# A hybrid decoder step on one core: its two prompt mixers cut into steps that are queued between the dense products

## Chip, cores and metric

The kernel runs on one core of a Trainium2 chip. Its time is the device time of one execution in microseconds (us); three executions were timed. An execution under the hardware profiler gives the trace that is read here. PE is TensorE, DVE VectorE, ACT ScalarE, POOL GpSimd, and SP is the engine that issues the DMAs.

## The reference

One layer of a hybrid decoder on 1024 prompt tokens and 8 sample tokens (one new token each, behind 4096 cached ones). Width 1024, all float32.

```python
def decoder_layer(x, s0, past_k, past_v, lb, lam, lam_init, p):
    h = x + 0.5 * swiglu(rmsnorm(x, p['ffn1_norm']), p['ffn1_w_gate'], p['ffn1_w_up'], p['ffn1_w_down'])
    z = rmsnorm(h, p['mix_norm']) @ p['w_in']
    xq, xf, xi, xg, dq, dk, dv = jnp.split(z, IN_SPLITS, axis=-1)
    o_hg, s_new = hgrn2_mixer(xq, xf, xi, xg, lb, s0, p['hg_out_norm'])
    q = rmsnorm(dq.reshape(B, L, 2 * DA_HEADS, DA_HEAD_DIM), p['da_q_norm'])
    k = rmsnorm(dk.reshape(B, L, 2 * DA_HEADS, DA_HEAD_DIM), p['da_k_norm'])
    v = dv.reshape(B, L, DA_HEADS, DA_VDIM)
    ...
    o_da = rmsnorm(o_da, p['da_subln']) * (1.0 - lam_init)
    o = jnp.concatenate([o_hg.reshape(B, L, HG_WIDTH), o_da.reshape(B, L, DA_WIDTH)], axis=-1).astype(dt)
    h = h + o @ p['w_out']
    y = h + 0.5 * swiglu(rmsnorm(h, p['ffn2_norm']), p['ffn2_w_gate'], p['ffn2_w_up'], p['ffn2_w_down'])
    return y, k, v, s_new
```

The mixer has two halves: a gated linear recurrence (HGRN2, 4 heads of 128, in blocks of tokens with a running state), and causal differential attention (4 heads, two softmax maps each, whose difference weighs the values). The sample tokens attend to a paged cache of 4096 keys and values each, and have a recurrent state of their own. `swiglu` has an inner width of 2816.

## The kernel before, in words

**Dense products.** Each float32 product is made in three passes on float32r operands (high and low parts of weights and activations: `split`, L106). `mm3` (L376) keeps a weight tile in TensorE and streams 256, 264 or 512 columns of tokens; `dstep` (L431) is the same for the FFN's way down, and `units` (L498) the input projection, where tokens are stationary and 256 weight columns stream. The weights come in 678 tiles of 256 KB (`wtile`, `wload`); ACT makes the high part of each and DVE, or every second time POOL while `shared[1]` is set, the low part.

**Stages.** The prompt goes in two groups of 512 tokens, group 0 as two slices of 256 and 264 columns (the 8 sample tokens ride in the second). `first_half(grp)` is FFN 1 and the input projection (`win_phase`), whose results go to DRAM scratch by name: hk, hv, hg, hq for the recurrence, aq, ak, av for the attention. `mixer(grp)` is the work of one group in both mixer halves: four blocks of 128 tokens through `hgrn_block`, then sixteen (head, block) units of `attention`. `second_half(grp)` is the output projection, FFN 2 and the way out. In time: first half of group 0; first half of group 1 beside mixer 0; second half of group 0 beside mixer 1; second half of group 1 alone. The sample rows (`sample_stream`: per token 32 pages of keys, a softmax, 32 pages of values; then their recurrence) run beside all from the middle of the first input projection on.

**A block of the recurrence.** For each of 8 units (4 heads, two halves q of the decay levels) `stage1` makes decays with two 512-column matmuls (L666, L667), an exponential on ACT (L668), and two products on DVE (L672, L673); `stage2` makes 3 or 4 level products (L699, with L692 in the first half) that DVE copies into place (hAT, L701 and L708), and in the second half of a head goes on to the values and the state (L713, L714, L716; then ACT L717, DVE L721 on `hst`). The block ends with a norm (ACT L734, DVE L737 and L197, POOL L198, DVE L741 on `hln`) and four transposes (L744). The factor of that norm is a power, taken on POOL (L198).

**A unit of the attention.** Scores of two maps (L786; DVE L788 and L792, ACT L793), their weighted difference (DVE L795 to L798), transposes (L809; ACT L810), values (L814), a norm (ACT L817 and L818, DVE L821 on `aos`) and a last transpose (L823).

**PSUM.** Three banks `mm` for the dense products, two `mx` (decays, scores), two `my` (everything else of the mixers) and one `nm`. A matmul that begins a bank's next tile waits until the engines that read the tile before last in `mx` or `my` are through.

**What sets the order.** Every engine executes its instructions in one fixed order, that a list scheduler makes while the program is built. The program hands it the work by `weave`: after each piece of dense work, which yields its own cost, the side streams are advanced as far as their credit goes (cost times a rate: `R0`, `R1` for the mixers, `S0` to `S2` for the sample rows). Mixer instructions are handed over with a priority of 3000 (`hp(3000)`), with which the scheduler may put them ahead of dense work that was handed over before them.

```python
    sstream[1] = S1
    shared[1] = True
    rest = weave(first_half(1, SBs), [[mixer(0), R0, 3000], sstream])
    for s in rest:
        if s is not sstream:
            run(s[0])
    sstream[1] = S2
    rest = weave(second_half(0, HA), [[mixer(1), R1, 3000]] + [s for s in rest if s is sstream])
    for s in rest:
        run(s[0])
    shared[1] = False
    run(second_half(1, HB))
```

Of the kernel before, what the change touches and what calls it, by code (L numbers as in the profile page):

```python
# [18 lines left out]
P = 128  # L19
# [9 lines left out]
# columns of the constant table  # L29
# [4 lines left out]
def shape_constants():  # L34
# [5 lines left out]
    for l in range(7):  # L40
# [6 lines left out]
        # the columns of right halves alone  # L47
# [12 lines left out]
def kernel(ctx: ExitStack, tc: tile.TileContext, I, O):  # L60
# [74 lines left out]
    def load_consts():  # L135
# [3 lines left out]
        # lower bound: c1n = -(1 - lb) / 2 with lb the softmax over the two rows  # L139
# [13 lines left out]
        # lambda  # L153
# [11 lines left out]
        # gains of the mixers  # L165
# [18 lines left out]
    # rows of the sample tokens  # L184
# [15 lines left out]
    class Group:  # L200
        """tokens that pass the weights together: tiles as wide as the group"""
# [9 lines left out]
    class Slice:  # L211
        """columns of a group that one matrix product takes"""
# [53 lines left out]
    def norm_sums(sl):  # L266
        """sums of squares by block, down the partitions; the columns of each height"""
# [6 lines left out]
    def norm_spread(sl, R, r):  # L274
        """the factors along a row, on all partitions"""
# [23 lines left out]
    def scaled(gi, sl, d):  # L299
        """what norm_finish makes, but for the norm's factors: those come with the products' results"""  # L300
# [6 lines left out]
    def norm_row(sl):  # L307
        """the factors alone, along a row"""
# [41 lines left out]
    def wload(H, L, raw, src):  # L350
        # while DVE has the most to do, some of the low parts on Pool
# [7 lines left out]
    def wtile(src, c):  # L359
        """c columns of weights, from tiles of 512 / c blocks of rows: pairs of (high, low) parts"""  # L360
# [18 lines left out]
    FB = [2, 4, 4, 4, 4, 4]  # L379

    def ffn(pre, slices, done, deferred=False):
        wg, wu, wd = (I[pre + n] for n in ("_w_gate", "_w_up", "_w_down"))

        def gateup(f, hs):
# [6 lines left out]
            def gate(sl):  # L391
                pg = MM()
                mm3(pg, G, sl)
# [10 lines left out]
            def up(sl):  # L404
                pu = MM()
                mm3(pu, U, sl)
# [8 lines left out]
            # by slices where what comes before goes by slices  # L415
# [4 lines left out]
            for fn, sl in order:  # L420
                fn(sl)
                yield 0.01 * sl.w

        def dstep(W, m, hs, d, sl):
# [3 lines left out]
            for j in range(m):  # L428
                (H, L), (hH, hL) = W[j], hs[sl][j]
                for q, (a, b) in enumerate(((H, hH), (H, hL), (L, hH))):  # L430
                    PE.matmul(ps[:, :w], a[:, cs], b[:, :w], start=j == 0 and q == 0, stop=j == m - 1 and q == 2)  # L431
# [828 lines left out]
```

## Time and profile before

| | us |
|---|---|
| median of 3 executions (2468.16 to 2472.86) | 2472.05 |
| span of the profiled execution, first to last instruction | 2471.9 |
| PE busy (matmul) | 2304.7 |
| DVE busy | 1827.5 |
| ACT busy | 1071.8 |
| POOL busy | 999.5 |
| mean granted TensorE clock, share of full speed | 0.971 |

The profiled execution's own time is its span, 2471.9 us; nothing outside it is given, and it lies 0.15 us under the median. A matmul's end is modelled in the trace and matmuls overlap, so that a busy PE may still do less work than it could: the number of matmuls in a stretch of time says more than its busy share.

### The profile page before, as it was taken

The numbers are of one execution on the slowest core, as the hardware profiler recorded it, in microseconds if no ns is written. First come the engines' busy times: TensorE is split into PE (matmuls) and PEld (weight loads), VectorE is DVE, ScalarE is ACT, GpSimd is POOL, SyncE is SP. The second block draws the span as 40 slices with busy tenths as digits, with TensorE's granted clock in tenths as the row PEclk, the third lists the DMA queues.
The fourth block names the chain that finished last, engine by engine and source line by source line (L and its number), as shares of the span: only waits on it lengthen the run. The fifth ranks groups of instructions, "written<-read, shape, count | busy, mean of one in ns | idle before, by whom it ended". The sixth has DMA issues, their size and how long they took to land. (4 is left out here: it accounts for less than half of the span.)

```text
span 2471.9 us, 44310 instructions
## 1 busy us (share of the span) xinstructions
PE 2304.7 (93%) x15101; PEld 2079.1 (84%) x15101; DVE 1827.5 (74%) x3750; ACT 1071.8 (43%) x2465; POOL 999.5 (40%) x788
## 2 busy tenths in 40 slices
PE   7999999989998978989899879889798999999999
PEld 6999999989877866767888767677687889999999
DVE  6555657596799796798798997997987766555554
ACT  4322324435544434545554643434465554322222
POOL 4100101381176374474684673785756310100000
PEclk9999999999998998999899999999999999999999
DMA  4332334684466467576785773566755652332332
GB/s 137 90 95 83 112 91 125 183 286 139 130 217 205 134 213 230 165 234 215 239 280 145 243 236 114 186 211 202 235 173 182 183 170 94 90 95 91 90 95 74
DMA packets 273396, 402.37 MB, mean 163 GB/s; under 512 B 29641, under 2 KB 104650, under 8 KB 273170
## 3 DMA queue, kind: packets, MB, share of 16 engines
q1 hardware_dynamic: 273170, 399.54, 52.0%
q8 instruction: 119, 1.95, 0.3%
q14 instruction: 107, 0.88, 0.1%
HBM read 361.22 MB, written 38.21 MB: 162 GB/s over the span
## 5 line engine op out<-in xcount | busy, mean ns | idle before, releaser
L376 PE MATMUL mm<-xn,wH 128*128 128x256 f32 (+2 forms) x4800 | 1121.8, 327 | 19.4 <-DVE xn L106 5.7
L376 PEld LDWEIGHTS mm<-xn,wH 128*128 128x128 f32 x4800 | 808.6, 192 | 94.8 <-DVE xn L106 8.1
L376 PE MATMUL mm<-xn,wL 128*128 128x256 f32 (+2 forms) x2400 | 782.7, 326 | 1.4 <-DVE wL L106 1.4
L106 ACT CAST wH<-wr 128x512 fp32r<-128x512 f32 x672 | 409.3, 617 | 518.1 <-PE mm L376 275.3
L106 DVE TENSOR_TENSOR wL<-wr,wH 128x512 fp32r<-128x512 f32 x504 | 414.7, 825 | 163.8 <-ACT wH L106 132.8
L431 PE MATMUL mm<-h,wH 128*128 128x264 f32 (+2 forms) x2112 | 487.0, 324 | 7.3 <-DVE ft L409 4.7
L376 PEld LDWEIGHTS mm<-xn,wL 128*128 128x128 f32 x2400 | 461.1, 192 | 36.8 <-DVE wL L106 1.8
L954 POOL TENSOR_TENSOR kv<-kv,ss 128x512 f32<-128x512 f32 x256 | 371.2, 1459 | 145.3 <-DMA kv<-in_cache_k 127.1
L431 PEld LDWEIGHTS mm<-h,wH 128*128 128x128 f32 x2112 | 349.9, 190 | 38.4 <-DVE ft L409 5.8
L411 POOL TENSOR_TENSOR ft<-ft,acc 128x256 f32<-128x256 f32 (+1 forms) x110 | 101.5, 922 | 656.6 <-DVE ft L409 645.9
L431 PE MATMUL mm<-h,wL 128*128 128x264 f32 (+2 forms) x1056 | 340.5, 323 | 0.0
L498 PE MATMUL mm<-wH,xn 128*128 128x256 f32 (+1 forms) x1728 | 325.5, 286 | 7.2 <-ACT ez L527 2.5
L106 POOL TENSOR_TENSOR wL<-wr,wH 128x512 fp32r<-128x512 f32 x168 | 237.9, 1417 | 223.0 <-ACT wH L106 184.7
L1004 DVE SCALAR_TENSOR_TENSOR sacc<-kv,sS,sacc 128x128 f32<-128x128 f32 x480 | 283.5, 645 | 20.4 <-POOL sacc L1008 20.4
L498 PEld LDWEIGHTS mm<-wH,xn 128*128 128x128 f32 (+1 forms) x1728 | 259.4, 180 | 17.5 <-ACT ez L527 3.2
L1006 ACT ACTIVATE kv<-kv,sS 128x128 f32<-128x128 f32 x512 | 164.5, 391 | 210.3 <-DMA kv<-in_cache_v 161.2
L498 PE MATMUL mm<-wL,xn 128*128 128x256 f32 (+1 forms) x864 | 246.2, 286 | 1.0 <-DVE wL L106 1.0
L1008 POOL TENSOR_TENSOR sacc<-sacc,kv 128x512 f32<-128x512 f32 x128 | 185.6, 1450 | 117.9 <-issue 27.3
L433 DVE SCALAR_TENSOR_TENSOR xr<-mm,xr 128x264 f32<-128x264 f32 (+2 forms) x288 | 146.0, 511 | 91.4 <-PE mm L431 91.0
L431 PEld LDWEIGHTS mm<-h,wL 128*128 128x128 f32 x1056 | 200.2, 190 | 14.7
L955 DVE TENSOR_REDUCE sS<-kv 128x8 f32<-128x512 f32 x256 | 170.8, 673 | 37.2 <-POOL kv L954 36.8
L498 PEld LDWEIGHTS mm<-wL,xn 128*128 128x128 f32 (+1 forms) x864 | 155.2, 180 | 4.7 <-DVE wL L106 1.2
(219 smaller groups left out, 2409.0 us busy)
## 6 DMA issues: line engine op xcount, KB each, us to landing
kv<-in_cache_k SPq DMA_DIRECT2D x256, 256.0 KB
kv<-in_cache_v SPq DMA_DIRECT2D x256, 256.0 KB
wr<-in_ffn_w_gate SPq DMA_DIRECT2D x176, 256.0 KB
wr<-in_ffn_w_up SPq DMA_DIRECT2D x176, 256.0 KB
wr<-in_ffn_w_down SPq DMA_DIRECT2D x176, 256.0 KB
wr<-in_w_in SPq DMA_DIRECT2D x96, 256.0 KB
aq<-qt SPq DMA_DIRECT2D x64, 128.0 KB
wr<-in_w_out SPq DMA_DIRECT2D x32, 256.0 KB
```

Of the source, the lines that this page charges most:

```text
L106: return ACT.copy(H, src), (eng or DVE).tensor_tensor(out=L, in0=src, in1=H.bitcast(F32), op=ALU.subtract)
L376: PE.matmul(ps[:, :w], a, b[k][:, :w], start=k == 0 and j == 0, stop=k == n - 1 and j == 2)
L411: POOL.tensor_tensor(out=t, in0=t, in1=sl.acc, op=ALU.mult)
L431: PE.matmul(ps[:, :w], a[:, cs], b[:, :w], start=j == 0 and q == 0, stop=j == m - 1 and q == 2)
L433: DVE.scalar_tensor_tensor(out=sl.xr[d][:, :w], in0=ps[:, :w], scalar=0.25, in1=sl.xr[d][:, :w], op0=ALU.mult, op1=ALU.add)
L498: PE.matmul(ps[:tb, 0:256], a, b, start=k == 0 and j == 0, stop=k == KC - 1 and j == 2)
L954: POOL.tensor_tensor(out=kt, in0=kt, in1=qb, op=ALU.mult)
L955: DVE.tensor_reduce(out=Sb[:, i], in_=kt.rearrange("p (n d) -> p n d", d=64), op=ALU.add, axis=AX.X)
L1004: DVE.scalar_tensor_tensor(out=acc[:, hs], in0=vt[:, hs], scalar=w, in1=acc[:, hs], op0=ALU.mult, op1=ALU.add)
L1006: ACT.activation(vt[:, hs], vt[:, hs], AF.Copy, scale=w)
L1008: POOL.tensor_tensor(out=acc, in0=acc, in1=vt, op=ALU.add)
```

## The change

The same instructions are issued, as many of each kind on each engine. What changes is the order in which the program hands them to the scheduler, some buffers, and one constraint:

- `mm3` yields once more half way, so that a dense product of 8 weight blocks has two places for side work, and `newest` is the dense matmul handed over last.
- In `weave`, a stream with a priority (the mixers) may advance by one step per place only, and its TensorE instructions are held behind `newest` in TensorE's order (`issue_after`, an order without a semaphore).
- The mixers are one stream `mixers()` over both groups, from the middle of group 0's input projection on, with one fixed cost per step (`HSTEP`, `ASTEP`). `wait_for` makes a step give its place up until a result of the input projection has been handed over; the recurrence needs "hk" and "hq", then "hv", then "hg".
- A block of the recurrence goes in three stages, each a step behind the one before; a block's last transposes go into the next block (`behind`), and `hln` has two buffers. A unit of the attention goes in four steps, interleaved with the unit before it, and the last transpose of a unit comes with the unit after the next.
- In group 1's input projection hq comes second instead of fourth (`WORDER`).

```diff
     def mm3(ps, W, sl):
         w = sl.w
         n = len(W)
         for k, (H, L) in enumerate(W):
             for j, (a, b) in enumerate(((H, sl.xH), (H, sl.xL), (L, sl.xH))):
-                PE.matmul(ps[:, :w], a, b[k][:, :w], start=k == 0 and j == 0, stop=k == n - 1 and j == 2)
+                newest[0] = PE.matmul(ps[:, :w], a, b[k][:, :w], start=k == 0 and j == 0, stop=k == n - 1 and j == 2)
+            if 2 * k + 2 == n:
+                yield 0.005 * w
...
+    def wait_for(name, grp):
+        while (name, grp) not in made:
+            yield WAIT
+
+    WAIT = -1.0
...
-    WORDER = [("aq", "ak", "hk", "hq", "hv", "hg", "av"), ("hk", "hv", "hg", "hq", "aq", "ak", "av")]
+    WORDER = [("aq", "ak", "hk", "hq", "hv", "hg", "av"), ("hk", "hq", "hv", "hg", "aq", "ak", "av")]
...
-    def hgrn_block(b):
+    def hgrn_block(b, STEP):
...
-        osb = TT("hln", [P, 512], bufs=1)
+        while behind:
+            behind.pop(0)()
+        yield STEP
+        osb = TT("hln", [P, 512], bufs=2)
...
-            if q == 0:
-                return
+        def stage3(h):
+            hs = slice(h * P, (h + 1) * P)
+            AT = live[h]
             po = MY()
...
+        yield from wait_for("hv", b // 4)
+        hv = TT("hvt", [P, 512], bufs=1)
+        SP.dma_start(hv, hv_d[b])
         units = [(h, q) for h in range(4) for q in range(2)]
-        for i in range(len(units) + DEEP):
+        for i in range(len(units) + 2):
+            if i >= 3 and i % 2:
+                stage3((i - 3) // 2)
+            if 0 < i <= len(units):
+                stage2(*units[i - 1])
             if i < len(units):
                 stage1(*units[i])
-            if i >= DEEP:
-                stage2(*units[i - DEEP])
             if i == HEAD and b % 4 < 3:
                 hgrn_head(b + 1)
-            yield 2.0
+            if i == HEAD + 1:
+                yield from wait_for("hg", b // 4)
+                gate = TT("s512", [P, 512], bufs=2)
+                SP.dma_start(gate, hg_d[b])
+            yield STEP
...
     def attention(grp):
         att_consts()
-        pend = None
-        for h in range(4):
-            KT, V = att_load(h, grp)
-            for b in range(4 * grp, 4 * grp + 4):
-                a, tn = yield from att_scores(h, b, KT)
-                if pend is not None:
-                    yield from att_values(*pend)
-                pend = (h, b, V, a, tn)
-        yield from att_values(*pend)
+        units = [(h, b) for h in range(4) for b in range(4 * grp, 4 * grp + 4)]
+        U, kv_of = [], {}
+        for k in range(len(units) + 2):
...
+            if k > 1:
+                att_out(*U[k - 2])
+            if k < len(units):
+                att_scores(h, b, KT, qx, w, 0)
+            yield ASTEP[grp]
+            if 0 < k <= len(units):
+                att_turn(*U[k - 1])
+                yield ASTEP[grp]
+            if k < len(units):
+                att_scores(h, b, KT, qx, w, 1)
+                yield ASTEP[grp]
+            if 0 < k <= len(units):
+                att_values(*U[k - 1])
+                yield ASTEP[grp]
...
+    def mixers():
+        for grp in range(2):
+            yield from wait_for("hk", grp)
+            with tc.tile_pool(name=f"hg{grp}", bufs=1) as top[0]:
+                hgrn_consts()
+                for i in range(4):
+                    yield from hgrn_block(4 * grp + i, HSTEP[grp])
+            yield from wait_for("all", grp)
+            with tc.tile_pool(name=f"at{grp}", bufs=1) as top[0]:
+                yield from attention(grp)
+            mixed[0] = grp + 1
+            yield 0.1
+
+    HSTEP = (5.1, 4.8)
+    ASTEP = (2.9, 3.4)
...
                 credit[i] += c * s[1]
                 while credit[i] > 0:
-                    with hp(s[2]):
+                    with hp(s[2]), tc.issue_after(newest[0].ins) if s[2] else nullcontext():
                         n = next(s[0], None)
...
-                    credit[i] -= n
+                    credit[i] = 0.0 if n == WAIT else credit[i] - n
+                    if s[2]:
+                        break
...
+    mstream = [mixers(), 1.0, 3000]
+    weave(main, [mstream, sstream])
     sstream[1] = S1
     shared[1] = True
-    rest = weave(first_half(1, SBs), [[mixer(0), R0, 3000], sstream])
...
+    weave(first_half(1, SBs), [mstream, sstream])
+    while mixed[0] < 1:
+        next(mstream[0])
     sstream[1] = S2
-    rest = weave(second_half(0, HA), [[mixer(1), R1, 3000]] + [s for s in rest if s is sstream])
-    for s in rest:
+    for s in weave(second_half(0, HA), [mstream, sstream]):
         run(s[0])
```

**The order at two places.** TensorE's order at the end of mixer 0's recurrence, the last head of its fourth block, before (dense products, L376 and L431, stand where rows are left out). my is the pair of banks; hXR and hE are the factors of the levels, hvt the values, hAT what DVE assembles, hln the block's result.

```order
L692 MATMUL my<-hqt,hkT 128x128
L716 MATMUL my<-hst,hqd 128x128
L699 MATMUL my<-hXR,hE 128x64 x3
...
L699 MATMUL my<-hXR,hE 128x64 x4
...
L713 MATMUL my<-hvt,hkt 128x128
...
L714 MATMUL my<-hvt,hAT 128x128
L716 MATMUL my<-hst,hqd 128x128
...
L744 MATMUL my<-ident,hln 128x128 x2
```

The same place in the changed kernel (L710, L717, L732, L733, L735 and L776 are the lines that were L692, L699, L713, L714, L716 and L744):

```order
L733 MATMUL my<-hvt,hAT 128x128
L735 MATMUL my<-hst,hqd 128x128
L710 MATMUL my<-hqt,hkT 128x128
L717 MATMUL my<-hXR,hE 128x64 x3
...
L717 MATMUL my<-hXR,hE 128x64 x4
L732 MATMUL my<-hvt,hkt 128x128
...
L733 MATMUL my<-hvt,hAT 128x128
L735 MATMUL my<-hst,hqd 128x128
...
L776 MATMUL my<-ident,hln 128x128 x2
```

The kinds follow each other as before. Between the last L716 and the first L744 stood 54 dense products, and now 40; L732 stands right behind the four level products where some dense rows lay between.

TensorE's order where mixer 1's recurrence begins, in group 1's input projection, before (L644, L645 and L650 open a block; L498 is the projection, L376 with 512 columns its hq part):

```order
L498 MATMUL mm<-wL,xn 128x256
L498 MATMUL mm<-wH,xn 128x256
L644 MATMUL mx<-hgL,sufr 128x512
L645 MATMUL mx<-hgH,sufr 128x512
L650 MATMUL mx<-ident,hkt 128x128 x4
...
L376 MATMUL mm<-xn,wH 128x512 x2
```

And in the changed kernel:

```order
L376 MATMUL mm<-xn,wH 128x512 x2
...
L502 MATMUL mm<-wL,xn 128x256
L660 MATMUL mx<-hgL,sufr 128x512
L661 MATMUL mx<-hgH,sufr 128x512
L666 MATMUL mx<-ident,hkt 128x128 x4
...
L502 MATMUL mm<-wH,xn 128x256 x2
```

The block's opening stood ahead of hq and now stands behind it: 6724 dense products precede it before, 7014 after. The recurrence of mixer 1, from its first decays (L666, now L684) to its last, lay over 1438 dense products and now lies over 1148; the attention that follows it begins 10 us of dense work earlier than before and ends at the same place.

## Rows read from the trace of the kernel before

**Rows 1.** Windows, three stages: us, busy (instructions) by engine, TensorE clock, DMA share, GB/s.

```profile
0.00:425.00 425.00, 409.20 (x3352) 405.18 (x3353) 254.36 (x528) 148.45 (x311) 66.05 (x88) 1.00 0.34 103
425.00:2035.00 1610.00, 1464.20 (x8176) 1245.07 (x8174) 1334.43 (x2739) 784.64 (x1877) 896.97 (x652) 0.96 0.63 198
2035.00:2471.90 436.90, 431.28 (x3575) 428.83 (x3575) 238.68 (x484) 138.71 (x279) 36.49 (x48) 1.00 0.30 91
```

**Rows 2.** Windows of 50 us within the second and third stage, columns PE, PEld, DVE, ACT, POOL.

```profile
700.00:750.00 50.00, 40.98 (x167) 32.66 (x166) 49.66 (x87) 19.96 (x50) 37.71 (x28) 0.88 0.68 223
800.00:850.00 50.00, 50.00 (x257) 41.73 (x256) 33.32 (x86) 22.99 (x55) 13.22 (x11) 1.00 0.37 111
850.00:900.00 50.00, 42.10 (x192) 33.83 (x191) 50.00 (x86) 18.75 (x48) 36.23 (x26) 0.93 0.64 208
1450.00:1500.00 50.00, 40.05 (x163) 31.53 (x162) 50.00 (x78) 21.98 (x44) 32.77 (x21) 0.86 0.58 183
1600.00:1650.00 50.00, 41.68 (x175) 34.25 (x176) 50.00 (x87) 19.09 (x49) 40.89 (x29) 0.86 0.63 205
```

**Rows 3.** Waits of PE, whole span: waiting line <- releaser: us in total, times, longest.

```profile
PE my L744 <- DVE hln L741: 15.3, 11, 4.1
PE my L699 <- DVE hst L721: 10.9, 4, 5.4
PE mx L786 <- DVE atn L788: 10.7, 7, 3.4
PE my L823 <- DVE aos L821: 10.1, 7, 2.4
PE my L714 <- DVE hAT L708: 8.1, 5, 3.5
...
PE my L713 <- DVE hAT L708: 6.1, 5, 3.6
...
PE mx L786 <- DVE atn L792: 5.9, 1, 5.9
PE mx L786 <- DMA aKT<-kt: 5.3, 2, 4.0
...
PE my L692 <- DVE hAT L708: 4.2, 2, 3.8
...
PE my L699 <- DVE hE L673: 3.9, 4, 1.4
...
PE mx L666 <- ACT s L647: 3.1, 2, 2.7
```

**Rows 4.** Timeline, end of the fourth block: start us, us, engine, line [idle before <-releaser].

```profile
919.89 0.67 DVE L737 TENSOR_REDUCE tiny<-s 128x4 f32<-128x512 f32 x1
...
921.68 0.47 DVE L197 TENSOR_SCALAR tiny<-tiny 128x4 f32<-128x4 f32 x1
922.08 2.60 POOL L954 TENSOR_TENSOR kv<-kv,ss 128x512 f32<-128x512 f32 x2
924.64 1.06 POOL L198 TENSOR_TENSOR tiny<-tiny,mhalf 128x4 f32<-128x4 f32 x1
...
928.91 0.34 PE L744 MATMUL my<-ident,hln 128*128 128x128 f32 x1 [3.15 <-DVE hln L741]
```

**Rows 5.** Groups by line, DVE: count, busy us, mean ns, idle before.

```profile
L1004 DVE SCALAR_TENSOR_TENSOR sacc<-kv,sS,sacc 128x128 f32<-128x128 f32 x480 | 283.5, 645 | 20.4 <-POOL sacc L1008 20.4
L955 DVE TENSOR_REDUCE sS<-kv 128x8 f32<-128x512 f32 x256 | 170.8, 673 | 37.2 <-POOL kv L954 36.8
...
L708 DVE COPY_PREDICATED hAT<-masks,my 128x64 f32<-128x64 uint8 x224 | 54.0, 241 | 9.5 <-PE my L699 7.5
L673 DVE TENSOR_TENSOR hE<-hE,hkT 128x384 f32<-128x384 f32 x64 | 52.1, 814 | 0.0
L672 DVE TENSOR_TENSOR hXR<-hE,hqt 128x384 f32<-128x384 f32 x64 | 51.1, 799 | 2.5 <-DMA hqt<-hq 1.2 <-PE my L699 1.0
...
L741 DVE SCALAR_TENSOR_TENSOR hln<-hln,tiny,s 128x128 f32<-128x128 f32 x32 | 21.6, 733 | 1.3 <-POOL tiny L198 1.1 <-DMA hvt<-hv 0.2
```

More of the change, by code (lines that the diff above doesn't have):

```diff
@@ L392, in gate @@
                 pg = MM()
-                mm3(pg, G, sl)
+                yield from mm3(pg, G, sl)
                 t = sl.view(tt)
@@ L405, in up @@
                 pu = MM()
-                mm3(pu, U, sl)
+                yield from mm3(pu, U, sl)
                 t = sl.view(tt)
@@ L420, in gateup @@
             for fn, sl in order:
-                fn(sl)
-                yield 0.01 * sl.w
+                yield from fn(sl)
+                yield 0.005 * sl.w
         def dstep(W, m, hs, d, sl):
@@ L430, in dstep @@
                 for q, (a, b) in enumerate(((H, hH), (H, hL), (L, hH))):
-                    PE.matmul(ps[:, :w], a[:, cs], b[:, :w], start=j == 0 and q == 0, stop=j == m - 1 and q == 2)
+                    newest[0] = PE.matmul(ps[:, :w], a[:, cs], b[:, :w], start=j == 0 and q == 0, stop=j == m - 1 and q == 2)
             with hp():
@@ L497, in units @@
                     for j, (a, b) in enumerate(((xH, WH), (xL, WH), (xH, WL))):
-                        PE.matmul(ps[:tb, 0:256], a, b, start=k == 0 and j == 0, stop=k == KC - 1 and j == 2)
+                        newest[0] = PE.matmul(ps[:tb, 0:256], a, b, start=k == 0 and j == 0, stop=k == KC - 1 and j == 2)
                 with hp():
@@ L506, in win_phase @@
                 yield from win_queries(slices)
+                made.add((name, grp))
                 continue
@@ L513, in win_phase @@
                 yield None
+            made.add((name, grp))
         turn(0)
-    WORDER = [("aq", "ak", "hk", "hq", "hv", "hg", "av"), ("hk", "hv", "hg", "hq", "aq", "ak", "av")]
+        made.add(("all", grp))
+    made = set()
+    def wait_for(name, grp):
[3 more added lines that the diff above has]
+    WORDER = [("aq", "ak", "hk", "hq", "hv", "hg", "av"), ("hk", "hq", "hv", "hg", "aq", "ak", "av")]
     NEZ = 4
@@ new lines, in att_scores @@
+        tn = w["tn"]
+        sb = w[j] = TT(f"ap{j}", [P, KT.shape[2]], bufs=2 - j)
+        for pc in range(npc):
+            m = min(512, n - pc * 512)
+            ps = MX()
+            for x in range(2):
+                PE.matmul(ps[:, :m], qx[:, j, x], KT[:, j, pc * 512:pc * 512 + m], start=x == 0, stop=x == 1)
+            r0 = (7 - b) * P + pc * 512
+            DVE.tensor_tensor_reduce(out=sb[:, pc * 512:pc * 512 + m], in0=ps[:, :m], in1=negrel[:, r0:r0 + m],
+                                     op0=ALU.add, op1=ALU.max, scale=SLOPES[h], scalar=-3e38, accum_out=tn[:, 2 * j + pc:2 * j + pc + 1])
@@ L1049, in wout_phase @@
             ps = MM()
-            mm3(ps, W[d], sl)
+            yield from mm3(ps, W[d], sl)
             with hp():
@@ L1134, in first_half @@
             yield c
-            if then is not None and i > 50:
+            if then is not None and i > 58:
                 next(then, None)
@@ L1153, in second_half @@
         yield from ffn("ffn2", slices, out_step, grp == 1 or len(slices) == 1)
-    def mixer(grp):
-        with tc.tile_pool(name=f"hg{grp}", bufs=1) as top[0]:
-            hgrn_consts()
-            for i in range(4):
-                yield from hgrn_block(4 * grp + i)
-        with tc.tile_pool(name=f"at{grp}", bufs=1) as top[0]:
-            yield from attention(grp)
+    mixed = [0]
+    def mixers():
[12 more added lines that the diff above has]
+    ASTEP = (2.9, 3.4)
     def run(g):
```

104 lines of the change are left out of this document (50 added, 54 removed).

## The prediction

> **What bounds the kernel now.** First the windows by stage [rows 1]. In the first 425 us and the last 437 us TensorE is busy to 96 and 99% at full clock, and VectorE to 60 and 55%: these 862 us are TensorE's own work, and the change leaves them alone. The 1610 us between, in which mixers and sample rows run beside the dense products, are where it acts. [...]
>
> Second the windows of 50 us [rows 2], which show that this stage alternates. From 800 to 850 TensorE is full at clock 1.00 with 257 matmuls and VectorE busy for 33 us: TensorE bounds. From 700 to 750, 850 to 900, 1450 to 1500 and 1600 to 1650 VectorE is busy for 49.7 to 50 us, TensorE passes 163 to 192 matmuls only, and its clock is 0.86 to 0.93: VectorE bounds. The two changes of hand cost time, since what one engine has to spare in one stretch does not help the other in the next.
>
> Third, what TensorE waits for [rows 3]. The eleven rows sum to 83.6 us, and all are mixer matmuls. Nine wait for VectorE: for the block's norm (L744), for a PSUM bank that VectorE still reads (L699, L713, L692, L786), for the assembled levels (L714) or the attention's norm (L823). One waits for a DMA, one for ScalarE. Dense products hardly wait at all. So TensorE stands in its fixed order before a mixer matmul whose input is late, with dense work behind it that could run.
>
> **Why an input is late** is seen at one place [rows 4]. The fourth block's norm has its sum of squares at 922.15 us. The power, 1.06 us on GpSimd, begins at 924.64, because two products of the sample rows (2.60 us) stand ahead of it in GpSimd's order. The first transpose starts at 928.91 after 3.15 us of idling. The sample rows also hold VectorE for 283.5 + 170.8 = 454 us [rows 5]. A longer pipeline gives more cover against such a delay, but takes none of the work away.
>
> **The change, part by part.** Instructions and their counts are the same on every engine, the DMAs too, so no busy time is added or removed. I read from the order how much TensorE work stands between the matmul whose result is worked on and the matmul that waits, and call it cover: a product of 256 columns at 0.12 us (431.3 us for 3575 matmuls in the last stage [rows 1]), one of 512 at nearly twice that, less the work on the result that VectorE's own order holds, at its rows' durations.
>
> *Waits of the mixers.* The median cover grows by 1.5 us for L744, 0.3 for L699 behind the state, 1.2 for L713, 0.7 for L714 and L692, 1.0 for L823, 1.6 for the banks of L786 and by 3.4 for those of L666. If each wait becomes shorter by that, at most by its mean [rows 3], it is: L744 11 x 1.39 = 15.3; L699 4 x 0.3 = 1.2; L713 5 x 1.2 = 6.0; L714 5 x 0.7 = 3.5; L692 2 x 0.7 = 1.4; L823 7 x 1.0 = 7.0; L786 10.7; L666 3.1; together 48 us. The waits for the keys' DMA (5.3), for the one late L792 (5.9) and for hE (3.9; this cover gets shorter, from some 25 to 10 us, and stays long) are left as they are. 48 us is the upper bound; the lower is nothing. For nothing speaks that the four full windows alone hold 9.0 + 7.9 + 10.0 + 8.3 = 35.2 of the 145.8 us of idling [rows 2]: where VectorE is full, TensorE waits a little later instead. And the L744 cover does not grow everywhere: at the place shown, in 54 dense products before and 40 now, it shrinks; the spread over the eight blocks narrows from 4.1 to 16.2 us to 7.7 to 11.9 us. I take the middle, -24.
>
> [...]
>
> [...]
>
> *The second recurrence is squeezed.* Its start does not come earlier. The scheduler, with the mixers' priority, had already put it into the input projection; now hq stands ahead of it and it starts 40 us of dense work later, ending at the same place: 222 us of dense work before, 182 now. The four largest of its VectorE lines make 54.0 + 52.1 + 51.1 + 21.6 = 178.8 us for eight blocks [rows 5], 89 for its four. 89 x (1 - 182/222) = 16 us of VectorE work more must fit into the shorter stretch. VectorE is busy for 83% of the stage [rows 1], so there is room on average but not in a full window. Bounds 0 and +16; I take the middle, +8, as the stage is made of both sorts of windows. The attention of mixer 1 gets 10 us more and needs nothing.
>
> *What costs nothing.* The head of hgrn_block loads hv and the gate later, close to their use; of the loads into a block only hqt shows up as a wait, at 1.2 us on VectorE [rows 5], and it is now issued a step ahead of its use. Weight loads keep their higher priority on SP and pass no more mixer DMAs than before. load_consts and the sample rows keep their places: the sample softmaxes stand within 10 us of dense work of where they stood. The second buffer of hln hides the transposes' read; without it the next block's first copy would wait for them.
>
> The profiled execution took 2471.9 us, 0.15 under the median: 2471.9 - 24 - 7 + 8 = 2448.9, and so **2449 us** for the median.
>
> **Rivals.**
>
> *Nothing moves, since the scheduler had made this pipeline already.* For it: at the places looked at the kinds of TensorE matmuls follow each other as before, and where VectorE is full the order of TensorE decides nothing. [...] Against it: the lower quartile of most covers grows. Time 2472, within 5.
>
> *Slower: the squeezed recurrence meets a full VectorE.* The 16 us come in whole, and the waits stay: 2472 + 16 = 2488. It decides if VectorE is busy for 48 of 50 us or more all through mixer 1's recurrence, where it now is between full windows and others. For it also: three of the four longest covers of L744 lose 4.9, 4.3 and 3.0 us, and at the last of these three the norm was late [rows 4].
>
> *All covers work.* The waits fall by 48 and the clock by 21, the recurrence finds room: 2472 - 48 - 21 = 2403. For it: the five largest waits are short, 1.4 to 2.7 us in the mean, and a few products more would cover them. Against: the full windows.
>
> **How the numbers follow.** A measurement of this kernel can tell about 0.2%, 5 us, from no change. The forecast (2436 to 2466) has a chance of 0.38, the larger gain 0.17, no change 0.15, slower 0.30. The last is high because the share of work that VectorE gets in its busiest stretches is, by the order, not smaller than before. So faster 0.55, same 0.15, slower 0.30. The range goes from just above the larger gain's time to just above the slower rival's, 2405 to 2490; the forecast's own bounds, -48 - 21 and +16, lie at 2403 and 2488.
>
> **What would show it.** Right: in the middle stage TensorE's idle time falls from 146 to about 120 us; L744's successor L776 waits for less than 8 us in all and the waits of L786's successor L815 on L788's fall by half; the mean clock rises from 0.971 to about 0.975; VectorE's busy time stays at some 1830 us in a shorter span. Wrong: idling that only changes its line, full VectorE windows between 1080 and 1450 us (the second recurrence), or a first stage that is not the same to a few us. A new wait that the order does not show, as on SP behind a mixer load, would also make it wrong.

## The result, and the profile after

The changed kernel takes **2512.75 us** in the median of 4 runs (2512.1 to 2517.02), 1.0169 of the kernel before (95% interval 1.0155 to 1.0184): 41 us slower, where 23 us faster was forecast, and outside the range.

The windows by stage, of the changed kernel (columns as in [rows 1]):

```profile
0.00:425.00 425.00, 407.32 (x3330) 403.33 (x3331) 251.29 (x524) 147.04 (x309) 66.38 (x87) 1.00 0.35 103
425.00:2035.00 1610.00, 1443.29 (x7963) 1222.09 (x7962) 1315.69 (x2681) 764.10 (x1835) 895.51 (x649) 0.95 0.63 194
2035.00:2511.00 476.00, 468.25 (x3812) 461.55 (x3810) 263.64 (x547) 159.36 (x323) 39.09 (x53) 1.00 0.33 97
```

The first stage is nearly as before [rows 1]. In the second TensorE passes 7963 matmuls in the 1610 us that held 8176, and 237 are left over for the third. Over the whole program:

```profile
span 2511.0 us, 44330 instructions
PE 2318.9 (92%) x15101; PEld 2087.0 (83%) x15101; DVE 1830.6 (73%) x3750; ACT 1070.5 (43%) x2465; POOL 1001.0 (40%) x788
```

The 39.1 us of span are 14.2 us that the same 15101 matmuls are busy for longer (mean granted clock 0.967, not 0.971) and 24.9 us more in which TensorE idles (2511.0 - 2318.9 = 192.1, before 2471.9 - 2304.7 = 167.2). VectorE does the same work in nearly the same time. So both things that the change was to reduce have grown. In the middle stage TensorE idles for 166.7 us (1610 - 1443.29); before it was 145.8 (1610 - 1464.20 [rows 1]), and about 120 was forecast. The waits of that stage that VectorE ended went from 112 to 132 us, all rows summed. What TensorE waits for in the whole span now, the longest rows:

```profile
PE my L856 <- DVE aos L852: 23.4, 8, 6.2
PE mm L435 <- DVE xr L437: 15.0, 10, 3.8
PE my L717 <- DVE hst L740: 11.8, 6, 4.9
PE my L776 <- DVE hln L769: 10.5, 8, 3.0
PE my L717 <- DVE hE L691: 10.2, 6, 3.1
PE my L733 <- DVE hAT L726: 9.6, 5, 3.9
PE mx L815 <- DVE atn L817: 8.6, 5, 2.4
PE my L732 <- DVE hAT L726: 6.7, 8, 2.1
```

Against [rows 3], the block's norm (L776, before L744) fell from 15.3 to 10.5 us and the scores' bank (L815, before L786) from 10.7 to 8.6. But the attention's last transpose (L856, before L823) went from 10.1 to 23.4, hE (now L717 behind L691) from 3.9 to 10.2, and a dense product, L435 of the FFN's way down, now waits 15.0 us; the answering row of before, L431 behind L433, had 2.0. The releaser is VectorE in all of them. The wait of L692 for hAT, 4.2 us, is gone.

**One such wait.** The longest, in the first attention; start, length, engine, line (of VectorE's queue the pieces behind 1259.68 us):

```profile
1260.54 0.28 ACT L849 ACTIVATE s<-my 128x128 f32<-128x128 f32 x1
1260.71 0.20 ACT L849 ACTIVATION_READ_ACCUMULATOR s<-my 128x1 f32 x1
```

```profile
1259.68 2.68 DVE L1058 SCALAR_TENSOR_TENSOR sacc<-kv,sS,sacc 128x128 f32<-128x128 f32 x4
1262.28 0.68 DVE L106 TENSOR_TENSOR wL<-wr,wH 128x512 fp32r<-128x512 f32 x1
1262.88 1.76 DVE L478 SCALAR_TENSOR_TENSOR ft<-ft 128x512 f32<-128x512 f32 x1
1264.57 0.14 DVE L197 TENSOR_SCALAR tiny<-atn 128x1 f32<-128x1 f32 x1
...
1265.22 2.48 DVE L1058 SCALAR_TENSOR_TENSOR sacc<-kv,sS,sacc 128x128 f32<-128x128 f32 x4
1267.63 0.67 DVE L1009 TENSOR_REDUCE sS<-kv 128x8 f32<-128x512 f32 x1
1268.22 1.06 DVE L852 TENSOR_SCALAR aos<-aos,tiny 128x128 f32<-128x128 f32 x1
```

```profile
1264.05 1.71 POOL L1008 TENSOR_TENSOR kv<-kv,ss 128x512 f32<-128x512 f32 x1
1265.73 0.59 POOL L198 TENSOR_TENSOR tiny<-tiny,mhalf 128x1 f32<-128x1 f32 x1
```

```profile
1269.43 0.45 PE L856 MATMUL my<-ident,aos 128*128 128x128 f32 x1 [6.18 <-DVE aos L852]
```

The sum of squares is there at 1260.91 us. The three steps that lead from it to `aos` take 0.14, 0.59 and 1.06 us, 1.8 in all, but they end at 1269.28, 8.4 us later: sample rows (L1008, L1009, L1058), a weight's low part (L106) and a pass over the queries of the dense hq product (L478) stand ahead of them in the queues of VectorE and GpSimd. TensorE comes to L856 with dense work behind it and idles for 6.18 us.

**Where along the program.** The dense products' matmuls (L376, L435 and L502, before L376, L431 and L498) are as many in both kernels, so time can be compared at the same count of them, from the start of each in the trace. Time of each kernel less that of the kernel before, in us; the last three columns are runs of the next section. A single wait just ahead of a count (the longest in the rows above is 6.2 us) moves its row:

| dense matmuls begun | before at | changed | finer weaving alone | rate 0.9 for pair 1 | changed, pace 1.6 |
|---|---|---|---|---|---|
| 4200 | 562 | +7.3 | +1.1 | -1.3 | +7.9 |
| 5700 | 965 | +11.3 | +3.2 | -6.2 | +12.0 |
| 6150 | 1102 | +1.7 | +0.5 | -5.8 | +10.2 |
| 6850 | 1252 | +33.9 | +12.0 | -7.5 | +22.3 |
| 7380 | 1358 | +17.4 | +9.2 | -8.1 | +26.2 |
| 7635 | 1414 | +17.6 | +12.2 | +12.6 | +22.8 |
| 8605 | 1743 | +41.5 | +27.7 | +20.3 | +38.5 |
| 9335 | 1997 | +38.8 | +26.2 | +19.6 | +34.6 |
| 9570 | 2052 | +39.1 | +27.6 | +16.7 | +26.0 |

A difference at one count is also a difference of place: at 6850 the changed kernel has just ended its first attention (last transpose at product 6849, before 6573) and not yet begun its second recurrence, which before had begun at 6750. Of the 39 us of span, 24 come between products 7635 and 8605, where the second pair of mixers meets the sample rows. That stretch, of the kernel before (972 dense matmuls) and of the changed one (975):

```profile
1413.90:1743.00 329.10, 291.14 (x1303) 232.15 (x1302) 295.52 (x547) 142.41 (x333) 219.16 (x153) 0.94 0.62 196
```

```profile
1431.80:1787.80 356.00, 303.16 (x1355) 240.42 (x1353) 322.01 (x594) 147.82 (x343) 232.95 (x162) 0.94 0.60 188
```

VectorE is busy for 90% in both, and the stretch is longer by 27 us with 26.5 us more of VectorE's work in it, at the same clock. Of that work 19 us are the sample rows' multiply-adds and reductions (L1004 and L955 before, L1058 and L1009 now: 104.5 and 123.6 us). The order has put it there.

### The profile page after: what moved, and what is told of

It reads as the page before. It is cut to its first block, busy times and chain, and to the rows that moved or that the text cites. A ratio compares the mean times of both kernels' runs of the same rounds, so it can differ in the third digit from the quotient of the medians.

```text
span 2511.0 us, 44330 instructions
## 1 busy us (share of the span) xinstructions
PE 2318.9 (92%) x15101; PEld 2087.0 (83%) x15101; DVE 1830.6 (73%) x3750; ACT 1070.5 (43%) x2465; POOL 1001.0 (40%) x788
## 5 line engine op out<-in xcount | busy, mean ns | idle before, releaser
L376 PE MATMUL mm<-xn,wH 128*128 128x256 f32 (+2 forms) x4800 | 1125.4, 329 | 18.6 <-DVE xn L106 6.6
L376 PEld LDWEIGHTS mm<-xn,wH 128*128 128x128 f32 x4800 | 813.0, 193 | 93.9 <-DVE xn L106 8.3
L376 PE MATMUL mm<-xn,wL 128*128 128x256 f32 (+2 forms) x2400 | 787.1, 328 | 0.0
L106 ACT CAST wH<-wr 128x512 fp32r<-128x512 f32 x672 | 409.8, 617 | 572.1 <-PE mm L376 317.6
L106 DVE TENSOR_TENSOR wL<-wr,wH 128x512 fp32r<-128x512 f32 x504 | 419.1, 834 | 174.2 <-ACT wH L106 139.7
L435 PE MATMUL mm<-h,wH 128*128 128x264 f32 (+2 forms) x2112 | 487.9, 325 | 21.3 <-DVE xr L437 15.0
L376 PEld LDWEIGHTS mm<-xn,wL 128*128 128x128 f32 x2400 | 463.5, 193 | 35.9
L1008 POOL TENSOR_TENSOR kv<-kv,ss 128x512 f32<-128x512 f32 x256 | 372.4, 1463 | 148.7 <-DMA kv<-in_cache_k 125.8
L435 PEld LDWEIGHTS mm<-h,wH 128*128 128x128 f32 x2112 | 350.3, 190 | 54.4 <-DVE xr L437 20.3
L435 PE MATMUL mm<-h,wL 128*128 128x264 f32 (+2 forms) x1056 | 342.5, 325 | 0.0
L502 PE MATMUL mm<-wH,xn 128*128 128x256 f32 (+1 forms) x1728 | 328.1, 288 | 9.0 <-DVE ez L558 2.3
L106 POOL TENSOR_TENSOR wL<-wr,wH 128x512 fp32r<-128x512 f32 x168 | 239.2, 1424 | 242.7 <-ACT wH L106 210.6
L1058 DVE SCALAR_TENSOR_TENSOR sacc<-kv,sS,sacc 128x128 f32<-128x128 f32 x480 | 284.7, 647 | 20.7 <-POOL sacc L1062 20.7
L502 PEld LDWEIGHTS mm<-wH,xn 128*128 128x128 f32 (+1 forms) x1728 | 261.6, 182 | 18.3 <-DVE ez L558 2.9
L502 PE MATMUL mm<-wL,xn 128*128 128x256 f32 (+1 forms) x864 | 247.6, 287 | 1.9 <-POOL wL L106 1.0
L435 PEld LDWEIGHTS mm<-h,wL 128*128 128x128 f32 x1056 | 200.7, 190 | 14.9
L1009 DVE TENSOR_REDUCE sS<-kv 128x8 f32<-128x512 f32 x256 | 170.4, 674 | 41.3 <-POOL kv L1008 41.3
L502 PEld LDWEIGHTS mm<-wL,xn 128*128 128x128 f32 (+1 forms) x864 | 156.7, 182 | 5.4 <-POOL wL L106 1.5
```

The costliest lines, as they stand in the source:

```text
L106: return ACT.copy(H, src), (eng or DVE).tensor_tensor(out=L, in0=src, in1=H.bitcast(F32), op=ALU.subtract)
L376: newest[0] = PE.matmul(ps[:, :w], a, b[k][:, :w], start=k == 0 and j == 0, stop=k == n - 1 and j == 2)
L435: newest[0] = PE.matmul(ps[:, :w], a[:, cs], b[:, :w], start=j == 0 and q == 0, stop=j == m - 1 and q == 2)
L502: newest[0] = PE.matmul(ps[:tb, 0:256], a, b, start=k == 0 and j == 0, stop=k == KC - 1 and j == 2)
L1008: POOL.tensor_tensor(out=kt, in0=kt, in1=qb, op=ALU.mult)
L1009: DVE.tensor_reduce(out=Sb[:, i], in_=kt.rearrange("p (n d) -> p n d", d=64), op=ALU.add, axis=AX.X)
```

## The experiments

Two theories first. Theory 1: VectorE's full windows make the loss, so less VectorE work removes it. Theory 2: the finer, paced pipeline itself costs. Differences are to runs of the kernel before on the same chip; the ratio's interval stands with each.

**Less work on VectorE**, in the kernel before and in the changed one; both leave out every second multiply-add of the sample values:

```diff
-                    DVE.scalar_tensor_tensor(out=acc[:, hs], ...
+                    if i % 4 == 0:
+                        DVE.scalar_tensor_tensor(out=acc[:, hs], ...
```

> The kernel before, without every second of the multiply-adds that VectorE does on the sample rows' values (256 of 480 at 0.645 us, 165 us of VectorE work; their pages' share is left out of the result). Theory 1 (full VectorE: the change moved VectorE work from stretches with room into stretches where VectorE has none, and the time followed it): the span falls by 60 to 140 us, since VectorE is no longer full. Theory 2 (the finer pipeline itself costs: more steps, each with a wait of its own): this kernel falls too, by some tens of us; what tells the theories apart is the distance to its twin.

> The changed kernel without the same 256 multiply-adds of VectorE (165 us; that share of the sample values is left out of the result). Theory 1: the distance to the kernel before with the same cut falls from 40 us to under 15. Theory 2: it stays between 30 and 50 us.

Measured: 2426.4 us (ratio 0.9806, 0.9785 to 0.9827) and 2469.4 us (0.9976, 0.9963 to 0.9989). With some 100 us of VectorE's busy time gone both gain 43 to 48 us, and the distance between them stays at 43. VectorE's work is worth half its length here, but it isn't the total that the change suffers from: theory 1 falls in this form.

**Undoing one part of the changed kernel.** The old order of the weights, and slower recurrence with faster attention:

```diff
-... ("hk", "hq", "hv", "hg", "aq", "ak", "av")]
+... ("hk", "hv", "hg", "hq", "aq", "ak", "av")]
```

> The changed kernel with group 1's input projection in the order of before (hk, hv, hg, hq). The second recurrence then begins some 13 us of dense work later still, ends 40 later, and the attention behind it is pressed into 190 instead of 232 us of dense work. Theory 1: the recurrence is less dense and the attention denser, whose VectorE work has room: 2500 to 2515. Theory 2: nothing changes, 2510 to 2516. A third theory, that the moved hq is what costs: back to 2475 to 2485.

```diff
-    HSTEP = (5.1, 4.8)
-    ASTEP = (2.9, 3.4)
+    HSTEP = (5.1, 5.6)
+    ASTEP = (2.9, 2.8)
```

> The changed kernel with other step costs for the second mixer alone: 5.6 instead of 4.8 for the recurrence, 2.8 instead of 3.4 for the attention. The second recurrence then lies over 230 instead of 192 us of dense work (237 before the change). Theory 1: the stretch from the output projection on, which took 27 us more, gives back half or more: 2485 to 2500. Theory 2: the pipeline is the same, 2508 to 2517.

Measured: 2523.7 us (1.0199, 1.0175 to 1.0223) and 2514.6 us (1.0162, 1.0141 to 1.0182). The early hq is not the cause: without it the changed kernel is 7 us slower by the ratios, 1.0199 and 1.0169, whose intervals overlap. With other rates the loss at product 8605 is 20 us in place of 42, but by product 9570, with the attention, it is 41. So a theory of one stretch alone falls.

Then faster hand-over, the old steps, and the old sequence of two stages:

```diff
-    mstream = [mixers(), 1.0, 3000]
+    mstream = [mixers(), 1.6, 3000]
```

> The changed kernel, with the mixers handed over 1.6 times as fast (1.6 units of their work for each unit of dense work, and not 1.0); the steps and their order inside a block or unit are as changed. By the order of TensorE the second recurrence then stands in 990 to 1149 us of dense work (changed: 1006 to 1198) and its attention ends at 1466 (changed: 1483). Theory A, the slow hand-over costs (mixers late, steps of one block too close together in dense work): most of the 40 us come back, 2470 to 2490. Theory B, the new steps themselves cost (second stage handed over before the next first stage, half scores, the late turn): no change, 2505 to 2520.

> The changed kernel with the steps of the kernel before inside the recurrence and the attention (hgrn_block and attention as they were, with waits for hq, hv and hg ahead of each block), the rest as changed: hand-over beside the input projection, one step per place, new order of the weights. Their costs are divided by the rates of the kernel before (0.55 and 0.8), so that they are handed over as fast as there. Theory A, start and pace of the hand-over cost: it stays slow, 2495 to 2520, since the first recurrence still starts at 543 us of dense work (changed 512, before 470). Theory B, the new steps cost: back to 2460 to 2480.

```diff
-            if 0 < i <= len(units):
-                stage2(*units[i - 1])
             if i < len(units):
                 stage1(*units[i])
+            if 0 < i <= len(units):
+                stage2(*units[i - 1])
```

> The changed kernel with one pair exchanged in the recurrence: the first stage of a unit is handed over before the second stage of the unit before it, as in the kernel before, and not after it. Theory B in its narrow form, the shorter way from the first stage to the second (cover for hE some 10 us and not 25) costs: the waits of the level products fall from 25.5 us towards 15 and the time by 10 to 20 us, 2492 to 2503. Theory A, pace and start: the scheduler moves little, 2507 to 2517.

Measured: 2500.1 us (1.0103, 1.0077 to 1.0130), 2509.0 us (1.0129, 1.0106 to 1.0153) and 2518.2 us (1.0161, 1.0136 to 1.0187). The pace is worth some 16 us by the ratios (1.0169 and 1.0103), 13 by the two spans; the old steps don't bring the old time back; the narrow theory of hE falls. In the run with pace 1.6 the three waits that had grown are shorter:

```profile
PE my L856 <- DVE aos L852: 11.1, 9, 3.2
...
PE my L717 <- DVE hE L691: 7.2, 4, 4.4
...
PE mm L435 <- DVE xr L437: 7.0, 8, 1.9
```

but the scores' bank and the block's norm wait longer again:

```profile
PE mx L815 <- DVE atn L817: 18.5, 16, 2.5
PE my L776 <- DVE hln L769: 17.4, 11, 3.8
```

The first three give back 23.3 us and the other two take 16.8. Nine of the table's 13 us come at the end, where the last attention ends 124 dense products earlier (its last transpose at product 9382, changed 9506). The stretch from product 9350 to about 9600, changed and with pace 1.6:

```profile
2041.70:2093.80 52.10, 48.83 (x346) 44.67 (x345) 29.57 (x76) 25.72 (x60) 1.65 (x3) 1.00 0.54 162
```

```profile
2038.20:2082.10 43.90, 42.15 (x299) 38.61 (x298) 22.27 (x43) 15.13 (x32) 0.55 (x1) 1.00 0.58 174
```

**One part alone, in the kernel before, and two parts undone.** hq second (the diff above, reversed):

> The kernel before with one part of the change alone: in the second input projection the queries of the recurrence (hq) come second and not fourth. In the changed kernel this part was worth 11 us (2523.7 without it, 2512.7 with it). By the order the second recurrence then stands in 964 to 1146 us of dense work (before 962 to 1199) and its attention ends 26 us earlier. Theory A, an early start and an early end of the mixers are what counts: faster, 2455 to 2468. Theory B, what is packed denser costs: 182 us of dense work for the second recurrence as in the changed kernel, so slower than 2480.

Changed kernel with pace 1.6 and the old order of the weights:

> The changed kernel with two parts undone: the mixers handed over 1.6 times as fast, and hq fourth in the second input projection as before. Only the new steps inside blocks and units, the weaving by single steps and the start of the first recurrence (517 us of dense work, before 501) remain; by the order both attentions then end where they ended before (941 and 1483). Theory A, pace (some 15 us by the run with the faster hand-over) and the early hq (13 us by the kernel before with that part alone) make the loss: 2473 to 2490. Theory B, the steps cost: the distance of the run with the faster hand-over stays or grows, 2495 to 2520.

New steps alone:

> The kernel before with one part of the change alone: the new steps of the recurrence and of the attention (second stage before the next first stage, third stage apart, scores by halves, turn and way out a unit later, loads close to their use). Hand-over, weaving and the order of the weights are as before. By the order the scheduler then runs the steps more quickly: second stages of the first recurrence in 501 to some 685 us of dense work (before 501 to 730), its attention ends at 914 (before 941), the second one at 1474 (before 1484). Theory B, the steps cost by themselves: 2495 to 2520. Theory A, only pace and place cost: within 2465 to 2485; by the packing of VectorE (the recurrence of group 0 in 45 us less of dense work) at the upper end or some 10 us above.

Finer weaving alone (also the two counts of places, 80 to 150 and 50 to 58, as in the change):

```diff
+            if 2 * k + 2 == n:
+                yield 0.005 * w
...
-            yield 0.01 * w
+            yield 0.005 * w
```

> The kernel before with one part of the change alone: dense products give way twice in each product of 24 matmuls and not once (finer weaving, which also moves the sample rows a little). Mixers stand within some 10 us of dense work of where they stood. All theories of the mixers' pace, place or steps: no change, 2468 to 2483. Theory D, the sample rows and what else stands beside are moved by the finer weaving and that costs: 2485 to 2500.

Finer weaving with the early hand-over and the old steps:

> The changed kernel with the steps of the kernel before and with hq fourth in the second input projection: finer weaving and the hand-over beside the input projection remain. By the order the first recurrence's second stages run from 549 to some 745 us of dense work (before 501 to 730), its attention ends at 973 (before 941), the second attention at 1475. Theory A, the later places of the mixers cost: 2495 to 2515, as with the early hq (2509). Theory B, the steps or the early hq: 2470 to 2485.

| run | us | ratio (95%) |
|---|---|---|
| hq second alone | 2487.2 | 1.0053 (1.0027 to 1.0079) |
| new steps alone | 2488.2 | 1.0063 (1.0045 to 1.0082) |
| finer weaving alone | 2500.8 | 1.0115 (1.0087 to 1.0142) |
| + early hand-over, one step per place, constraint behind `newest` | 2503.4 | 1.0123 (1.0097 to 1.0148) |
| + new steps, pace 1.6 | 2506.5 | 1.0117 (1.0097 to 1.0137) |
| + hq second | 2500.1 | 1.0103 (1.0077 to 1.0130) |
| + pace 1.0 = the change | 2512.8 | 1.0169 (1.0155 to 1.0184) |

From the fourth row on each run adds to the one above. Finer weaving, which I had not priced, costs 28 us; early hand-over, new steps and hq then add nothing that can be told from it; the pace adds 16. Yet hq and the new steps, put into the kernel before by themselves, cost 13 and 16 us: parts don't add up.

Nor are the waits the same. With the finer weaving alone the matmuls are busy for 14.5 us longer and TensorE idles for 13.0 us more, but over the span the waits that VectorE ended fell from 115 to 105 us, and those that ScalarE ended rose from 23 to 41. Two of them:

```profile
PE mx L668 <- ACT hE L670: 13.4, 5, 4.4
...
PE my L816 <- ACT aaT L812: 8.6, 5, 4.3
```

The first product of the decays waited for ScalarE for 3.1 us before (L666, [rows 3]), the values for 2.8:

```profile
PE my L814 <- ACT aaT L810: 2.8, 2, 2.0
```

ScalarE had mostly been held up itself. The longest wait of L668:

```profile
1499.19 0.63 ACT L253 ACTIVATE xt<-xr 128x512 f32<-128x512 f32 x1 [4.54 <-DVE xr L1054]
1499.84 1.28 ACT L670 ACT_TABLE_LOAD   x1
1501.13 0.60 ACT L670 ACTIVATE hE<-mx 128x512 f32<-128x512 f32 x1
```

```profile
1501.79 0.80 PE L668 MATMUL mx<-Mr,hgL 128*128 128x512 f32 x1 [4.42 <-ACT hE L670]
```

The exponential's input was there at 1492.23 us, but L253 stood ahead of it and waited 4.54 us for VectorE. In three of the five waits of L668, 9.0 of the 13.4 us, an instruction ahead in ScalarE's queue had waited 4.3 to 5.5 us for VectorE; ahead of the longest wait for `aaT` (4.3 us) ScalarE had waited 7.8 us for a DMA. So a delay on VectorE also reaches TensorE through a third engine's queue.

**Edits that are no part of the change.** If each part costs about as much as any other, perhaps any shift of the order does. Three shifts were run; both changed rates of the mixers are faster ones, no slower one was tried.

```diff
-    R0, R1 = 0.55, 0.8
+    R0, R1 = 0.8, 1.2
```

> The kernel before with its two rates of hand-over changed from 0.55 and 0.8 to 0.8 and 1.2. By the order this moves the second stages by 0 to 14 us of dense work and the ends of the attentions by 0 to 5, which no theory gives a price. It shows how much the time moves by small shifts of place alone: if they are worth nothing, 2468 to 2483; if every small shift is a new draw, up to 15 us to either side.

The same with `R0, R1 = 0.55, 0.9`, and the sample rows' `S2` at 0.80 in the kernel before and in the changed one:

> The kernel before with the rate of the second pair of mixers 0.9 and not 0.8. By the order the second recurrence then ends at 1207 us of dense work and not 1234, its attention at 1475 and not 1484. Theory E: 2480 to 2500. If an earlier end of the second pair is a gain in itself (it was -7 to -12 us behind product 9500 in three runs): 2455 to 2470.

> The kernel before with the sample rows' rate in the last third of their way 0.80 and not 0.85. Instructions up to the second recurrence stand as before; after it the mixers shift by 0 to 4 us of dense work, and the sample rows by more. Theory E, the kernel before stands in a narrow best place and any shift of order costs: 2480 to 2500, all of it behind product 7500. Otherwise: 2466 to 2478.

> The changed kernel with the same shift of the sample rows, 0.80 and not 0.85. Theory E: the changed kernel is one of many places, some better and some worse, so within 15 us of 2512 to either side. If the changed kernel's loss is mainly an unlucky place, the shift can give back 20 us or more: below 2492.

Measured: both rates 2496.0 us (1.0086, 1.0060 to 1.0112); R1 alone 2493.8 us (1.0078, 1.0061 to 1.0095); S2 2478.7 us (1.0016, 1.0001 to 1.0031) in the kernel before and 2513.0 us (1.0148, 1.0131 to 1.0165) in the changed one. Handing over the second pair of mixers faster, or both pairs, costs 19 to 21 us without any part of the change; a slower rate for the sample rows costs some 4. In the changed kernel that rate gives back 5 us by the ratios, whose intervals overlap, and not the 20 that I had set as the sign of an unlucky place. With R1 at 0.9 the loss comes in one stretch, from 8 us ahead at product 7380 to 13 behind at 7635; the kernel before (255 dense matmuls) and this run (250):

```profile
1357.60:1413.90 56.30, 49.46 (x383) 47.04 (x382) 54.38 (x129) 35.55 (x86) 35.73 (x26) 0.97 0.73 232
```

```profile
1352.00:1429.60 77.60, 57.02 (x363) 51.01 (x361) 77.01 (x145) 41.29 (x100) 58.47 (x43) 0.85 0.80 250
```

GpSimd is busy for 58.47 us and not 35.73: more of the sample rows lies beside the recurrence (single key products stand up to 186 dense products earlier than before), VectorE has 77.01 us of work in place of 54.38, 16.5 of the 22.6 us more being sample rows, and about as many dense matmuls take as long as VectorE does, at clock 0.85. With both rates raised the loss comes elsewhere: 7 us at product 7635, 10 at 8110 and 23 at 8605.

**Looking for a better version.** Keys and queries of the first recurrence earlier, in the kernel before:

```diff
-    WORDER = [("aq", "ak", "hk", "hq", "hv", "hg", "av"), ...
+    WORDER = [("hk", "hq", "aq", "ak", "hv", "hg", "av"), ...
```

> The kernel before with keys and queries of the first recurrence (hk, hq) made first in the first input projection, ahead of aq and ak. The first recurrence's second stages then begin at 433 us of dense work and not 501, and the last attention ends at 1474 and not 1484. Theory A, what counts is how thin the mixers are spread over dense work: 40 us earlier at one end for 41 us of time is the measure of the change, so up to 60 us here, 2420 to 2465. Theory B, an early start is worth nothing by itself: 2465 to 2485.

And with hv and hg ahead too:

> The kernel before with hk, hq, hv and hg ahead of aq, ak and av in the first input projection. The first recurrence stands in 432 to some 590 us of dense work (before 501 to 730) and its attention in 653 to 836 (before 777 to 941), so that both are packed closer, with dense work alone behind them; the second group stays. Theory A, spread and pace count: slower, 2480 to 2510. Theory B, a late start was what cost: faster, 2440 to 2465.

Measured: 2489.7 us (1.0053, 1.0036 to 1.0069) and 2542.9 us (1.0265, 1.0248 to 1.0282). The first is 24 us ahead at product 6150 and 9 behind at 7380. The second is 49 us behind at product 4900, where recurrence 0 is packed closer, wins back 42 by 5700, and loses 45 between 6150 and 7380. No order that was run beats the kernel before.

## Why the prediction was wrong

**The step that failed is the waits' term, -24 us.** I took the order's cover (TensorE work between a result and its use, in the median) and let each wait shorten by its growth. The rows of this term sum to 68.5 us before and to 72.1 now, where 44.5 was forecast. The two largest terms have the right sign and too large a size: the norm's wait fell by 4.8 us of 15.3 (I asked for less than 8 in all; 10.5 are left), the scores' bank by 2.1 of 10.7 (I asked for half). Three waits for hAT and the state, with covers said to grow by 0.3 to 1.2 us, did not fall (L713, L714 and L699 before, L732, L733 and L717 now); only L692's 4.2 us went. L823's cover grew by 1.0 us in the median and its wait by 13.3. The cover of hE, which shrank to 10 us but "stays long", cost 6.3 more, and L435, which I didn't look at, 13.0. That "dense products hardly wait at all" I had read from a choice of rows that left them out: in the middle stage their bank held 33.7 us of the 145.8 before, and 44.3 now. A result's delay is not a property of TensorE's order. In the wait shown, 1.8 us of work took 8.4 us through two queues, more than the cover. Even the lower bound that I gave the term, nothing, was too good: the waits changed line and grew.

**The clock, -7 us**, fell with it. No run shows these 7 us, nor the 21 us of the bound and of the rival in which all covers work; in their place the changed kernel's mean clock is 0.967 and not 0.975, that of the middle stage 0.95 with 166.7 us of idling (0.96 with 145.8 before [rows 1]), and 14.2 us of busy time are lost.

**The squeezed second recurrence, +8 us**, can't be told apart in the result. It stands at products 7036 to 8184 now, and there the loss grows from 23 to 35 us; but counted from 6750, where it began before, it grows by 2 us only, and the end of the first attention lies in between. My price was a share of the recurrence's own VectorE work. What counts is what else lies in the same stretch: R1 at 0.9 moved the same recurrence and added 21 us in some 250 products, most of it by sample rows beside it. The rival "slower" had this mechanism at 16 us, but its condition (VectorE busy 48 of 50 us all through) was not met:

```profile
1450.00:1500.00 50.00, 41.28 (x187) 32.18 (x187) 49.97 (x83) 24.36 (x59) 38.28 (x28) 0.97 0.66 207
1500.00:1550.00 50.00, 41.49 (x175) 32.73 (x173) 43.74 (x78) 17.84 (x29) 25.54 (x17) 0.86 0.48 149
1550.00:1600.00 50.00, 47.55 (x235) 38.85 (x234) 42.81 (x93) 23.71 (x61) 27.39 (x20) 0.98 0.45 137
1600.00:1650.00 50.00, 41.51 (x174) 33.26 (x173) 49.97 (x87) 18.97 (x48) 39.75 (x27) 0.88 0.62 201
```

Full windows alternate with others as before [rows 2], and in the window from 1500 to 1550 TensorE idles for 8.5 us though VectorE has room. The stretch that I named for this sign, 1080 to 1450 us, was not the second recurrence's: the decays of the second recurrence run from 1239 to 1612 us in the trace of the kernel before and from 1313 to 1646 now.

**What I costed at nothing.** The finer weaving has no place in my sum, as it adds no instruction; alone it costs 28 us. The sample rows "keep their places", I wrote, their softmaxes within 10 us of dense work. In the trace of the changed kernel single key products stand up to 186 dense products earlier (6748, before 6934), some 22 us at 0.12 us each by my estimate; in the run with R1 at 0.9, which costs 19 us, they moved as far. The pace (1.0 unit of mixer cost per unit of dense work) costs 16 us; I had read it as part of the cover.

**What is shown and what is open.** Shown: TensorE's idling grew by 25 us, the rows of the waits' term grew where they were to shrink, in the changed kernel the growth lies in waits for VectorE, no part that was run alone is a gain, and rates of hand-over that are no part of the change cost 19 to 21 us. No neighbour that was run is better than the order of the kernel before. Argued only: that the 28 us of the finer weaving come from the order, since it adds no instruction; 9 us of its waits are traced to VectorE by way of ScalarE's queue, the rest is not. Not tried: the changed kernel without the finer weaving, or without the constraint behind `newest`; every run of the changed kernel has that constraint, and the three in the table cost within 3 us of the finer weaving alone. Open is what makes the order before so good between products 7380 and 8605, beyond the one collision with the sample rows that is shown.

## What to carry to other kernels

Where two engines are both near full (here TensorE 91% and VectorE 83% of the middle stage before, 90 and 82% after), a new order of the same instructions is a new packing. Its price can't be read from the cover at single waits: compare, over each stretch of the main work, what every other engine's queue holds there before and after, and count an unrelated shift's cost (here up to 21 us, 0.9%) as the least uncertainty on either side. Before believing a part of such a change, run a control that shifts the order without it.

## What the runs showed that I had not expected

VectorE's busy time was not the same for the same instructions. The 504 subtractions that make weights' low parts took 414.7 us in the kernel before and 429.2 with the finer weaving alone:

```profile
L106 DVE TENSOR_TENSOR wL<-wr,wH 128x512 fp32r<-128x512 f32 x504 | 414.7, 825 | 163.8 <-ACT wH L106 132.8 <-PE mm L431 14.1 <-PE mm L498 4.8
```

```profile
L106 DVE TENSOR_TENSOR wL<-wr,wH 128x512 fp32r<-128x512 f32 x504 | 429.2, 853 | 167.5 <-ACT wH L106 139.8 <-PE mm L433 13.3 <-PE mm L500 1.9
```

That is 28 ns more for each. These are two single traces; whether two of one kernel differ as much, and what makes the difference, was not tried.
